# State-space work of a hybrid decoder step: loads three slots behind their stores, and state, output and gated products in one slot

## The chip, the cores and the metric

The kernel runs on one core of a Trainium2 chip. The metric is device time in microseconds (us); 1889.3 us is the median of three runs before the change, 1888.42 to 1891.9.

## The reference

One step of a decoder layer on 256 prompt tokens and 8 x 4 sample tokens, 288 token columns in all: a gated feed-forward block, a mixer of two branches side by side, and a second feed-forward block. The change is in the first branch, the state-space model (SSM), with 64 groups of 16 channels and 64 complex states each.

```python
x = x + 0.5 * swiglu(rms_norm(x, ffn1_norm), ffn1_w_gate, ffn1_w_up, ffn1_w_down)
u, q, k, v = split(rms_norm(x, mix_norm) @ w_in)
# SSM branch, s5_mixer:
bu = einsum('blgc,gpc->blgp', u, B_bar);  bu[:, 0] += lam_bar * h0
_, h = associative_scan(h_t = lam_bar * h_{t-1} + bu_t)
y = gelu(einsum('blgp,gcp->blgc', h, C).real + D * u)
y_ssm = y * sigmoid(einsum('blgc,gcd->blgd', y, w_glu))
# attention branch: sliding window of 128, 16 query heads on 4 key heads
x = x + w_out @ concat(rms_norm(y_ssm), rms_norm(y_attn))
x = x + 0.5 * swiglu(rms_norm(x, ffn2_norm), ...)
```

The last states h and the new key and value rows are outputs too.

## The kernel before

**Pieces and slots.** All large products read their weights in pieces of up to 512 KB. For each piece the weight is split into two parts (wh by ScalarE, line 104; wl by VectorE, line 105), and three products (lines 288 to 290) of 288 columns are made for each of 8 row blocks: 24 products a piece. Making one piece's products is a *slot*; the mixer's slots are counted here from its first piece (*base* = slot 0). Slots 0 to 39 are the input projection (two slots for each 128 columns: key, then eight pieces j = 0 to 7 of u, key, value twice, eight pieces of q), slots 40 to 71 the output projection.

**What sets the order.** Every engine runs its instructions in the order in which the program issues them. At the start of slot n, `W.next` issues the split of piece n+2 (wh and wl have three buffers each, so this split waits until the products of piece n-1 are through), the load of piece n+5 (raw, on the SP queue), and then the list of other work hung on slot n: `W.at(slot, f)` hangs one call on a slot, `W.spread(slot, gen)` runs one step of a generator in each slot from there on. Then come the slot's 24 products. So TensorE does the small products hung on slot n first and the 24 products after them, and VectorE does the wl of piece n+2 first and then the slot's other work. Calls hung before stand ahead of calls hung later; steps of a generator are hung when the step before has run.

**The SSM branch.** For each j, with s = base + 2j + 5: the projected u is scaled by VectorE (line 714) and stored to DRAM as ud (`ssm_u_store`, on ScalarE's queue), and loaded back in another layout as U (`ssm_u_load`, four DMAs on the SP queue). Tables are loaded from DRAM: ma (for the state), rot, mb (for the output), and the decay row D0 is built. `ssm_state` is a generator of four steps: (1) 8 products of U and ma (L748) and four VectorE products with rot (L754 to L757); (2) sums and the two scans (L760 to L766); (3) ScalarE and POOL prepare the rest, and VectorE rotates back into cs (L775, L776); (4) VectorE finishes cs (L778, L779). `ssm_out` makes 12 products from U, cs and mb (L788 to L790) and the gelu yg; `ssm_y_store` and `ssm_y_load` take it through DRAM (yd) into yn; `ssm_glu` makes the gated product (L809), a tanh, y2 (L814), and its split into hh and hl with the sum of squares acc (L699, L703). The norm of the branch (line 222 with ones and acc, then VectorE) gives R_ssm, which the output projection's results need from slot 40 on. `state_done` and `ssm_done` close pools whose memory the attention then uses; `cache_k_load` and `cache_v_load` load into it.

Each fp32 product of small tiles appears in the profile as two instructions (the 8 of L748 as 16). All PSUM tiles come from eight buffers named main.

Of the kernel before, what the change touches and what calls it, by code (L numbers as in the profile page):

```python
# [10 lines left out]
F32 = mybir.dt.float32  # L11
# [6 lines left out]
P = 128  # L18
# [6 lines left out]
W1 = NB + NCH  # L25
# [7 lines left out]
EPS = 1e-6  # L33
# [99 lines left out]
def tile_hymba_step(ctx, tc, io):  # L133
# [499 lines left out]
    with ExitStack() as es:  # L633
        mix(tc, nc, io, es, W, MIX0, dict(
            x=x, xh=xh, xl=xl, gains=gains, ident=ident, ones=ones, acc=acc, R=R, tp=tp,
            dr=dr, pm=pm, pa=pa, proj=proj, mm3=mm3, norm=norm, rsqrt=rsqrt, now=now, Hold=Hold,
            mats=mats, e4=e4, h4=h4, h0=h0, post=post_norm(32)))
# [9 lines left out]
def mix(tc, nc, io, es, W, base, e):  # L647
    act, dve, pool_e, pe = nc.scalar, nc.vector, nc.gpsimd, nc.tensor
    tt, ts, stt = dve.tensor_tensor, dve.tensor_scalar, dve.scalar_tensor_tensor
    x, R, gains, ident, acc = e["x"], e["R"], e["gains"], e["ident"], e["acc"]  # L650
# [6 lines left out]
    sa = sa_es.enter_context(tc.tile_pool(name="ssm_in", bufs=1, side="right", reuse_waits="tile"))  # L657
    sm = sb_es.enter_context(tc.tile_pool(name="ssm_out", bufs=1, reuse_waits="tile"))
    late = {}

    def aux():
        return pa.tile([P, 512], F32, name="main")
# [7 lines left out]
    R_ssm = mp.tile([P, N], F32, name="R_ssm")  # L670
# [16 lines left out]
    def y_split(pool, src, g, first, eng=pool_e):  # L687
        hh = pool.tile([P, N], F32R, name="hh", bufs=8)
        if first:
            pool.tile([P, 32], F32, name="gap_y", bufs=1)  # L690
        hl = pool.tile([P, N], F32R, name="hl", bufs=8)
        gc = gains[:, g:g + 1]
        act.activation(halved(hh), evens(src), AF.Copy, scale=gc)
        YH.append(hh)
        YL.append(hl)
        sq = tp.tile([P, N], F32, name="sq", bufs=3)
        act.activation(sq, src, AF.Square)
        yield
        stt(halved(hl), evens(src), gc, halved(hh.bitcast(F32)), op0=ALU.mult, op1=ALU.subtract)  # L699
        if first:  # L700
            eng.tensor_copy(acc, sq)
        else:
            eng.tensor_tensor(acc, acc, sq, op=ALU.add)  # L703


    MA, MB, ROT, D0, U, CS, UE, YG, YN, GL = ({} for _ in range(10))
    c4 = [P, 4, NCH]

    def flat(ap):
        return ap.rearrange("p q k -> p (q k)")  # L710
# [20 lines left out]
        get(ROT[j].rearrange("p q s k -> p (q s k)"), e["mats"][j][:, 2560:])  # L731

    def ssm_decay(j):
        D0[j] = sa.tile(c4, F32, name="d0", bufs=2)
        act.copy(D0[j], e["e4"][:, 4 * j:4 * j + 4, None].to_broadcast(c4))
        pool_e.memset(D0[j][:, :, 0:1], 0.0)

# [4 lines left out]
    def ssm_state(j):  # L742
        ma, u, rot = MA.pop(j), U[j], ROT.pop(j)
        b = []
        for i in range(2):
            ps = aux()
            for q in range(4):
                pe.matmul(ps[:, q * W1:(q + 1) * W1], ma[:, i, q], u[:, q], start=True, stop=True)  # L748
            b.append(ps[:, :N].rearrange("p (q t) -> p q t", q=4))
        br, bi = b[0][:, :, NB:], b[1][:, :, NB:]  # L750
        co, si = rot[:, :, 0, :], rot[:, :, 1, :]
        a1, a2, a3, a4 = (sa.tile(c4, F32, name="ra%d" % i, bufs=2) for i in range(4))
        q = slice(4 * j, 4 * j + 4)
        tt(a1, br, co, op=ALU.mult)  # L754
        tt(a2, bi, si, op=ALU.mult)
        tt(a3, bi, co, op=ALU.mult)
        tt(a4, br, si, op=ALU.mult)  # L757
        yield
        for i in range(2):
            tt(fin_s[:, i, q, :], b[i][:, :, :NB], fin_s[:, i, q, :], op=ALU.add)  # L760
        tt(a1, a1, a2, op=ALU.add)
        tt(a3, a3, a4, op=ALU.subtract)
        d0 = flat(D0.pop(j))
        zr, zi = a2, a4
        dve.tensor_tensor_scan(flat(zr), d0, flat(a1), 0.0, op0=ALU.mult, op1=ALU.add)
        dve.tensor_tensor_scan(flat(zi), d0, flat(a3), 0.0, op0=ALU.mult, op1=ALU.add)  # L766
        yield
        cs = CS[j] = sm.tile([P, 2, 4, W1 + 1], F32, name="cs", bufs=2)
        pool_e.memset(cs[:, :, :, NB:NB + 1], 0.0)
        act.copy(cs[:, 0, :, :NB], e["h0"][:, 0, q, :])  # L770
        act.copy(cs[:, 1, :, :NB], e["h0"][:, 1, q, :])
        sr, si_ = cs[:, 0, :, NB + 1:], cs[:, 1, :, NB + 1:]
        pool_e.tensor_tensor(a1, zi, si, op=ALU.mult)
        pool_e.tensor_tensor(a3, zr, si, op=ALU.mult)
        tt(sr, zr, co, op=ALU.mult)  # L775
        tt(si_, zi, co, op=ALU.mult)  # L776
        yield
        tt(sr, sr, a1, op=ALU.subtract)  # L778
        tt(si_, si_, a3, op=ALU.add)  # L779
        for i in range(2):  # L780
            pool_e.tensor_copy(fin[:, i, q], cs[:, i, :, W1])

    def ssm_out(j):
        mb, u, cs = MB.pop(j), U.pop(j), CS.pop(j)
        ps = aux()
        for q in range(4):
            o = ps[:, q * W1:(q + 1) * W1]
            pe.matmul(o, mb[:, 0, q], u[:, q], start=True, stop=False)  # L788
            pe.matmul(o, mb[:, 1, q], cs[:, 0, q, :W1], start=False, stop=False)  # L789
            pe.matmul(o, mb[:, 2, q], cs[:, 1, q, :W1], start=False, stop=True)  # L790
        YG[j] = sm.tile([P, 4, W1], F32, name="yg", bufs=1)
        act.activation(YG[j].rearrange("p q t -> p (q t)"), ps[:, :N], AF.Gelu_apprx_tanh)

    def ssm_y_store(j):
# [11 lines left out]
    def ssm_glu(j):  # L806
        yn = YN.pop(j)
        ps = aux()
        pe.matmul(ps[:, :N], GL.pop(j), yn, start=True, stop=True)  # L809
        t = tp.tile([P, N], F32, name="s1")  # L810
        act.activation(t, ps[:, :N], AF.Tanh, scale=0.5)
        yield
        y2 = tp.tile([P, N], F32, name="s2")
        stt(y2, t, 1.0, yn, op0=ALU.add, op1=ALU.mult)  # L814
        yield
        yield from y_split(ys, y2, 48 + j, j == 0, dve if j == 7 else pool_e)
# [14 lines left out]
    for j in range(8):  # L831
        s = base + 2 * j + 5
        W.at(s, ssm_u_store, j)
        W.at(s, ssm_load_a, j)
        W.at(s + 2, ssm_u_load, j)
        W.at(s + 2, ssm_decay, j)
        W.at(s + 2, ssm_load_r, j)
        W.spread(s + 4, ssm_state(j), True)
        W.at(s + 6, ssm_load_b, j)
        W.at(s + 9, ssm_out, j)  # L840
        W.at(s + 10, ssm_y_store, j)
        W.at(s + 11, ssm_y_load, j)
        W.spread(s + 13, ssm_glu(j))
    W.at(s + 8, state_done)
    W.at(s + 17, ssm_done)
    W.spread(s + 18, e["norm"](e["ones"], acc, R_ssm, 1.0 / 1024, 4 * EPS))

    def tok(ap, blk):

# [236 lines left out]
    for i in range(8):  # L1086
        s = base + 2 * (12 + i) + 2
# [3 lines left out]
        W.at(s + 11, pv, i)  # L1091
    for p in range(2):
        s = base + 2 * (12 + 4 * p + 3) + 2
        W.at(s - 4, cache_k_load, p)
        W.at(s + 4, cache_v_load, p)
        W.at(s, cache_gain, p)
        W.spread(s + 2, sample(p))
    for i in range(8):
        p, g = divmod(i, 4)
# [186 lines left out]
```

## Time and profile before

| | us |
|---|---|
| median of three runs | 1889.3 (1888.42 to 1891.9) |
| the profiled execution | 1890.48 |
| its span, first to last instruction | 1888.7 |
| TensorE (PE) busy in the span | 1864.6 |
| VectorE (DVE) busy | 1208.9 |
| ScalarE (ACT) busy | 850.2 |
| GpSimd (POOL) busy | 301.1 |
| mixer: start of slot 0, of slot 40 | 805.31, 991.98 |

Times in the profile count from the first instruction. A timeline row gives start, duration, engine, line, operation, result<-operands, shapes and count, and in brackets the engine's idle time before it with what ended it. A row of the waits gives engine and line, what was waited for, the total in us, how often, and the longest. A SPq or ACTq row is the issue of DMAs by that queue, and its duration includes what the queue waited for. Starts of two rows of one engine, subtracted, give the pace; a product's own duration overlaps with the next. Lines from 738 on carry the same numbers in both kernels up to L822; behind it the changed kernel's are 6 higher.

### The profile page before, as it was taken

To read this page: it belongs to the slowest core of one execution; us is meant where nothing else is said; L and a number is where in the kernel's file an instruction comes from. 1 tells how busy PE (TensorE), PEld (TensorE's weight loads), DVE (VectorE), ACT (ScalarE), POOL (GpSimd) and SP (SyncE) were. 2 spreads that over 40 slices of the span, in tenths; PEclk is the share of its full clock that TensorE was granted. 3 is DMA by queue.
4 is the path that set the end of the run, shared out by engine and by line. 5 is a ranking of instruction groups with operands and counts; after the bars stand their busy time and mean duration, and the time that the engine had idled before them with its cause. 6 is when DMAs were issued, how large, how long until landed. Compare 5 with 4: busy or idle time off the path is not lost.

```text
span 1888.7 us, 37634 instructions
## 1 busy us (share of the span) xinstructions
PE 1864.6 (99%) x15256; PEld 1850.5 (98%) x15256; DVE 1208.9 (64%) x1874; ACT 850.2 (45%) x1334; POOL 301.1 (16%) x450
## 2 busy tenths in 40 slices
PE   7999999999999999999999999999999999999999
PEld 7999999999999999999988999999999999999999
DVE  5677767666667755687788885555555555555555
ACT  6444444544444444643477554443444334434443
POOL 3111011000200100211378650000000000000000
PEclk9999999999999999999999999999999999999999
DMA  7565656557665765778743456555655565556555
GB/s 244 185 195 166 215 182 213 194 167 232 202 202 162 226 212 151 237 248 276 248 140 122 158 172 187 180 163 182 195 174 180 168 195 182 168 163 207 179 162 168
DMA packets 122623, 359.04 MB, mean 190 GB/s; under 512 B 22449, under 2 KB 30257, under 8 KB 121265
## 3 DMA queue, kind: packets, MB, share of 16 engines
q1 hardware_dynamic: 114672, 340.81, 57.6%
q10 hardware_dynamic: 7776, 15.83, 2.5%
q8 instruction: 119, 1.95, 0.4%
q14 instruction: 56, 0.45, 0.1%
HBM read 338.40 MB, written 20.22 MB: 190 GB/s over the span
## 4 chain that ended last, share of the span: by engine, by line
PE 92%; DVE 2%; POOL 2%; DMA 1%; ACT 1%; issue 1%; SPq 0%; POOLq 0%; ACTq 0%; DVEq 0%
PE main L288 30%; PE main L290 30%; PE main L289 29%; DVE wl L105 1%; ACT wh L104 1%; PE main L748 1%; DMA U<-ud 0%; DMA ud<-t 0%; POOL acc L206 0%; PE main L581 0%; PE main L587 0%; POOL x L1111 0%; DMA raw<-in_w_gu 0%; PE main L789 0%; PE main L790 0%
## 5 line engine op out<-in xcount | busy, mean ns | idle before, releaser
L105 DVE TENSOR_TENSOR wl<-raw,wh 128x1024 fp32r<-128x1024 f32 (+2 forms) x680 | 756.1, 1112 | 466.4 <-ACT wh L104 461.5
L288 PE MATMUL main<-xh,wh 128*128 128x288 f32 x3136 | 904.4, 288 | 7.0 <-ACT xh L196 6.4
L290 PE MATMUL main<-xh,wl 128*128 128x288 f32 x3136 | 898.6, 287 | 3.0 <-DVE wl L105 3.0
L289 PE MATMUL main<-xl,wh 128*128 128x288 f32 x3136 | 898.4, 286 | 0.6 <-DVE xl L197 0.6
L104 ACT CAST wh<-raw 128x1024 fp32r<-128x1024 f32 (+2 forms) x680 | 639.6, 942 | 510.4 <-PE main L289 349.7
L288 PEld LDWEIGHTS main<-xh,wh 128*128 128x128 f32 x3136 | 594.2, 189 | 8.6 <-ACT xh L196 6.4
L290 PEld LDWEIGHTS main<-xh,wl 128*128 128x128 f32 x3136 | 593.9, 189 | 3.9 <-DVE wl L105 3.9
L289 PEld LDWEIGHTS main<-xl,wh 128*128 128x128 f32 x3136 | 594.1, 189 | 1.4 <-DVE xl L197 0.9
L288 PE MATMUL main<-hh,wh 128*128 128x288 f32 x1664 | 478.0, 287 | 1.3 <-DVE t L1110 0.7
L289 PE MATMUL main<-hl,wh 128*128 128x288 f32 x1664 | 476.0, 286 | 0.6 <-DVE hl L699 0.6
L290 PE MATMUL main<-hh,wl 128*128 128x288 f32 x1664 | 476.0, 286 | 0.0
L288 PEld LDWEIGHTS main<-hh,wh 128*128 128x128 f32 x1664 | 314.5, 189 | 1.9 <-DVE t L1110 0.9
L289 PEld LDWEIGHTS main<-hl,wh 128*128 128x128 f32 x1664 | 314.5, 189 | 1.0 <-DVE hl L699 0.8
L290 PEld LDWEIGHTS main<-hh,wl 128*128 128x128 f32 x1664 | 314.5, 189 | 0.2 <-DVE wl L105 0.2
L315 POOL TENSOR_TENSOR s<-s,R 128x288 f32<-128x288 f32 x88 | 70.5, 801 | 1144.6 <-ACT s L314 1144.6
L314 ACT ACTIVATE s<-t 128x288 f32<-128x288 f32 x88 | 39.0, 443 | 220.8 <-DVE t L313 220.8
L324 ACT CAST hh<-h 128x288 fp32r<-128x288 f32 x88 | 38.0, 432 | 221.9 <-DVE h L323 221.9
L345 DVE SCALAR_TENSOR_TENSOR x<-main,x 128x288 f32<-128x288 f32 x128 | 58.4, 456 | 39.9 <-PE main L290 39.6
L323 DVE TENSOR_TENSOR h<-main,s 128x288 f32<-128x288 f32 x88 | 40.1, 455 | 55.5 <-PE main L290 55.1
L313 DVE TENSOR_TENSOR t<-main,R 128x288 f32<-128x288 f32 x88 | 40.1, 456 | 45.7 <-PE main L290 45.4
L325 DVE TENSOR_TENSOR hl<-h,hh 128x288 fp32r<-128x288 f32 x88 | 40.3, 458 | 43.8 <-ACT hh L324 43.8
L206 POOL TENSOR_TENSOR acc<-acc,sq 128x288 f32<-128x288 f32 x45 | 44.9, 999 | 41.5 <-ACT sq L202 40.1
(266 smaller groups left out, 901.3 us busy)
## 6 DMA issues: line engine op xcount, KB each, us to landing
raw<-in_w_gu SPq DMA_DIRECT2D x352, 512.0 KB, 3.8
raw<-in_w_dn SPq DMA_DIRECT2D x128, 384.0 KB, 3.1
raw<-in_w_dn SPq DMA_DIRECT2D x128, 320.0 KB, 3.1
raw<-in_w_in SPq DMA_DIRECT2D x40, 512.0 KB, 4.5
raw<-in_w_out SPq DMA_DIRECT2D x32, 512.0 KB, 3.4
mats<-stage ACTq DMA_DIRECT2D x8, 1536.0 KB, 7.2
mb<-mats SPq DMA_DIRECT2D x8, 768.0 KB, 7.0
ma<-mats SPq DMA_DIRECT2D x8, 512.0 KB, 4.1
```

What stands on the lines that cost most here:

```text
L104: self.nc.scalar.copy(wh[:, :n], t[:, :n])
L105: self.nc.vector.tensor_tensor(wl[:, :n], t[:, :n], wh[:, :n].bitcast(F32), op=ALU.subtract)
L206: eng.tensor_tensor(acc, acc, sq, op=ALU.add)
L288: pe.matmul(ps, wh[:, s], woven(rh[k]), start=first and a == 0, stop=False)
L289: pe.matmul(ps, wh[:, s], woven(rl[k]), start=False, stop=False)
L290: pe.matmul(ps, wl[:, s], woven(rh[k]), start=False, stop=last and a == n - 1)
L313: dve.tensor_tensor(t1, pg[:, :N], R, op=ALU.mult)
L314: act.activation(s1, t1, AF.Silu)
L315: pool_e.tensor_tensor(s2, s1, R, op=ALU.mult)
L323: dve.tensor_tensor(halved(h), evens(pu[:, :N]), evens(s2), op=ALU.mult)
L325: dve.tensor_tensor(hl, h, hh.bitcast(F32), op=ALU.subtract)
L345: dve.scalar_tensor_tensor(x[d], ps[:, :N], 0.5, x[d], op0=ALU.mult, op1=ALU.add)
```

## The change

The SSM's steps are hung on later slots. Relative to s: U's load moves from 2 to 3, ma from 0 to 4, rot from 2 to 5, the decay row from 2 to 6, the state's four steps from 4..7 to 6..9, mb from 6 to 8, the output from 9 to 10, yd's store from 10 to 11, yn's load from 11 to 14, the gated product's four steps from 13..16 to 16..19. The norm takes two slots (39 and 40) instead of four (37 to 40). D0 has one buffer instead of two, yg two instead of one; the attention's cache loads are one slot later.

```diff
-        D0[j] = sa.tile(c4, F32, name="d0", bufs=2)
+        D0[j] = sa.tile(c4, F32, name="d0", bufs=1)
...
-        YG[j] = sm.tile([P, 4, W1], F32, name="yg", bufs=1)
+        YG[j] = sm.tile([P, 4, W1], F32, name="yg", bufs=2)
...
         W.at(s, ssm_u_store, j)
-        W.at(s, ssm_load_a, j)
-        W.at(s + 2, ssm_u_load, j)
-        W.at(s + 2, ssm_decay, j)
-        W.at(s + 2, ssm_load_r, j)
-        W.spread(s + 4, ssm_state(j), True)
-        W.at(s + 6, ssm_load_b, j)
-        W.at(s + 9, ssm_out, j)
-        W.at(s + 10, ssm_y_store, j)
-        W.at(s + 11, ssm_y_load, j)
-        W.spread(s + 13, ssm_glu(j))
-    W.at(s + 8, state_done)
-    W.at(s + 17, ssm_done)
-    W.spread(s + 18, e["norm"](e["ones"], acc, R_ssm, 1.0 / 1024, 4 * EPS))
+        W.at(s + 3, ssm_u_load, j)
+        W.at(s + 4, ssm_load_a, j)
+        W.at(s + 5, ssm_load_r, j)
+        W.at(s + 6, ssm_decay, j)
+        W.at(s + 8, ssm_load_b, j)
+        W.at(s + 10, ssm_out, j)
+        W.at(s + 11, ssm_y_store, j)
+        W.at(s + 14, ssm_y_load, j)
+        W.spread(s + 16, ssm_glu(j))
+        W.spread(s + 6, ssm_state(j))
+    W.at(s + 10, state_done)
+    W.at(s + 18, ssm_done)
+
+    def ssm_norm():
+        for n, _ in enumerate(e["norm"](e["ones"], acc, R_ssm, 1.0 / 1024, 4 * EPS)):
+            if n == 1:
+                yield
+
+    W.spread(s + 20, ssm_norm())
...
-        W.at(s - 4, cache_k_load, p)
-        W.at(s + 4, cache_v_load, p)
+        W.at(s - 3, cache_k_load, p)
+        W.at(s + 5, cache_v_load, p)
```

What that does to the order is seen at three places. On VectorE, before, from the split of slot 12 to that of slot 13 (j = 0 in its fourth step, j = 1 in its second; the number behind ra tells them apart):

```order
L105 TENSOR_TENSOR wl<-raw,wh 128x1024
L778 TENSOR_TENSOR cs<-cs,ra_10473 128x4x64
L779 TENSOR_TENSOR cs<-cs,ra_10475 128x4x64
L760 TENSOR_TENSOR h_210<-main,h_210 128x32 x2
L761 TENSOR_TENSOR ra_10584<-ra_10584,ra_10585 128x256
L762 TENSOR_TENSOR ra_10586<-ra_10586,ra_10587 128x256
L765 SCALAR_TENSOR_TENSOR ra_10585<-d_10452,ra_10584 128x256
L766 SCALAR_TENSOR_TENSOR ra_10587<-d_10452,ra_10586 128x256
L105 TENSOR_TENSOR wl<-raw,wh 128x1024
```

The same stretch in the changed kernel, slot 14:

```order
L105 TENSOR_TENSOR wl<-raw,wh 128x1024
L760 TENSOR_TENSOR h_210<-main,h_210 128x32 x2
L761 TENSOR_TENSOR ra_10630<-ra_10630,ra_10631 128x256
L762 TENSOR_TENSOR ra_10632<-ra_10632,ra_10633 128x256
L765 SCALAR_TENSOR_TENSOR ra_10631<-d_10617,ra_10630 128x256
L766 SCALAR_TENSOR_TENSOR ra_10633<-d_10617,ra_10632 128x256
L778 TENSOR_TENSOR cs<-cs,ra_10528 128x4x64
L779 TENSOR_TENSOR cs<-cs,ra_10530 128x4x64
L105 TENSOR_TENSOR wl<-raw,wh 128x1024
```

The fourth step of j now stands behind the second step of j + 1. On TensorE, before, the end of slot 13 and the first output (j = 0, slot 14), followed by slot 14's own products:

```order
L290 MATMUL main<-xh_102,wl 128x288
L788 MATMUL main<-U,mb 128x72
L789 MATMUL main<-cs,mb 128x72
L790 MATMUL main<-cs,mb 128x72
L788 MATMUL main<-U,mb 128x72
L789 MATMUL main<-cs,mb 128x72
L790 MATMUL main<-cs,mb 128x72
```

And in the changed kernel the end of that first output, now in slot 15, with what follows it:

```order
L788 MATMUL main<-U,mb 128x72
L789 MATMUL main<-cs,mb 128x72
L790 MATMUL main<-cs,mb 128x72
L748 MATMUL main<-U,ma 128x72 x8
L288 MATMUL main<-xh_95,wh 128x288
L289 MATMUL main<-xl_112,wh 128x288
```

Before, a state (of j + 3) came one slot behind the output; now the state of j + 2 (L748) stands right behind it in the same slot. From j = 3 the gated product L809 of j - 3 stands ahead of the output (before, from j = 2, that of j - 2). On the SP queue, before, at the first U loads:

```order
L96 DMA raw<-in_w_in 128x1024 x2
L723 DMA U<-ud_10084 32x4x72 x4
L731 DMA rot<-mats_198 128x512
L727 DMA ma<-mats_199 128x1024
L96 DMA raw<-in_w_in 128x1024 x2
L723 DMA U<-ud_10085 32x4x72 x4
```

And in the changed kernel:

```order
L723 DMA U<-ud_10084 32x4x72 x4
L96 DMA raw<-in_w_in 128x1024
L727 DMA ma<-mats_198 128x1024
L96 DMA raw<-in_w_in 128x1024
L731 DMA rot<-mats_198 128x512
L723 DMA U<-ud_10085 32x4x72 x4
L96 DMA raw<-in_w_in 128x1024
```

A weight load now stands between any two groups of SSM loads, where two stood behind a longer group.

## The prediction

> **What bounds the kernel now.** First the page's busy shares, then who TensorE waited for.
>
> ```profile
> span 1888.7 us, 37634 instructions
> PE 1864.6 (99%) x15256; PEld 1850.5 (98%) x15256; DVE 1208.9 (64%) x1874; ACT 850.2 (45%) x1334; POOL 301.1 (16%) x450
> ```
>
> TensorE is busy for all but 24.1 us of the span, so a change that leaves its work alone acts only through its pauses. The table of its waits lists them:
>
> ```profile
> PE main L288 <- ACT xh L196: 6.4, 1, 6.4
> PE main L748 <- DMA U<-ud: 2.6, 3, 1.3
> PE main L748 <- DVE wl L105: 2.3, 1, 2.3
> PE main L990 <- POOL lg L942: 1.5, 2, 1.0
> PE main L961 <- DVE rq_v L1026: 1.4, 1, 1.4
> ```
>
> The 6.4 us are the start. The SSM's own share is the two rows of L748, the state product, which waits for its reloaded input U: 4.9 us. The attention (L990, L961) has about 3 us more.
>
> The third look is at windows of one slot each (columns: stretch, its length, busy time of each engine, granted clock, DMA share, GB/s): one slot of 24 main products, the state products of one j with nothing else, the output products of one j.
>
> ```profile
> 830.26:833.20 2.94, 2.94 (x27) 2.94 (x25) 2.87 (x6) 1.05 (x1) 0.00 (x0) 1.00 0.81 278
> 833.20:834.90 1.70, 1.70 (x18) 1.70 (x17) 1.67 (x3) 1.35 (x2) 0.10 (x1) 1.00 1.04 328
> 854.38:857.06 2.68, 2.68 (x28) 2.68 (x26) 2.36 (x5) 2.33 (x2) 0.00 (x0) 1.00 1.01 384
> ```
>
> So a slot of main products is 2.94 us, the state adds 1.70, the output about 2.6. These are TensorE's own time and the change keeps all of it. DMA is full here (1.01 to 1.04 in two of the three). The timelines of the SP queue and of TensorE, and the SP queue's waits, show why U is late:
>
> ```profile
> 850.75 8.20 SPq L723 DMA_DIRECT2D U<-ud  x4
> 860.00 0.86 SPq L96 DMA_DIRECT2D raw<-in_w_in  x2
> SPq L802 <- DMA yd<-yg: 16.8, 4, 6.6
> SPq L723 <- DMA ud<-t: 8.7, 2, 6.4
> 870.94 0.29 PE L290 MATMUL main<-xh,wl 128*128 128x288 f32 x1
> 873.55 2.51 PE L748 MATMUL main<-U,ma 128*128 128x72 f32 x16 [2.33 <-DVE wl L105]
> 875.81 0.59 PE L288 MATMUL main<-xh,wh 128*128 128x288 f32 x1
> ```
>
> SP issues the U load right after the store and stands on its landing (8.20 us for four issues), with weight loads queued behind. The worst result is the 2.33 us pause before 873.55. Its row names wl, but the other states don't wait for wl, and U was being loaded; I read it as U.
>
> **What the change removes.** U is now loaded three slots behind its store and used three slots later; yn likewise. SP runs ahead of TensorE, but the rot load, which now waits for VectorE's work on j - 3 and stands ahead of U in SP's order, holds it back to about one slot ahead; two slots then remain between the store and the load, 5.9 us of main products plus one group of SSM products, and three slots between the load and its use. The longest stand was 8.20 us, so I take the 4.9 us as gone. Each pause also costs a restart: the state that waited 0.97 us (row below) lengthened its slot from 845.59 to 851.44, 5.85 us against 2.94 + 1.70 = 4.64, so 0.24 more than the wait; four of these are 1.0. And the big pause was followed by a slow stretch:
>
> ```profile
> 849.66 1.98 PE L748 MATMUL main<-U,ma 128*128 128x72 f32 x16 [0.97 <-DMA U<-ud]
> 851.44 0.37 PE L288 MATMUL main<-xh,wh 128*128 128x288 f32 x1
> 871.40:874.82 3.42, 1.27 (x12) 1.30 (x12) 2.04 (x4) 1.53 (x4) 0.62 (x3) 1.00 1.06 291
> 874.82:878.23 3.41, 3.41 (x17) 3.41 (x17) 1.36 (x4) 0.00 (x0) 0.92 (x2) 0.50 0.95 308
> 878.23:881.65 3.42, 3.42 (x28) 3.24 (x27) 0.94 (x2) 1.35 (x2) 0.00 (x0) 1.00 0.99 340
> ```
>
> After 3.42 us in which TensorE was busy for 1.27, the granted clock was 0.50 for 3.41 us: 1.7 us lost. Removed in all: 4.9 + 1.0 + 1.7 = 7.6 us. Ends: 3.6 (if the pause at 873.55 is a wait for wl that stays) and 7.6.
>
> **What it adds: the output now follows its state's last step by one slot.** Before, L778 and L779 (the last step, which finishes cs) ran in slot s+7 and the output in s+9; now s+9 and s+10. And on VectorE the last step of j now stands behind the scan step of j+1 (L760 to L766), which stood behind it before. VectorE, ScalarE and TensorE in slot 12 of before:
>
> ```profile
> 845.59 0.29 PE L288 MATMUL main<-xh,wh 128*128 128x288 f32 x1
> 845.73 1.05 ACT L104 CAST wh<-raw 128x1024 fp32r<-128x1024 f32 x1 [2.51 <-PE main L289]
> 846.88 1.21 DVE L105 TENSOR_TENSOR wl<-raw,wh 128x1024 fp32r<-128x1024 f32 x1
> 848.01 0.41 DVE L778 TENSOR_TENSOR cs<-cs,ra 128x256 f32<-128x256 f32 x1
> 848.35 0.41 DVE L779 TENSOR_TENSOR cs<-cs,ra 128x256 f32<-128x256 f32 x1
> 848.68 0.27 DVE L760 TENSOR_TENSOR h<-main,h 128x32 f32<-128x32 f32 x2
> 850.15 0.66 DVE L766 TENSOR_TENSOR_SCAN ra<-d,ra 128x256 f32<-128x256 f32 x1
> 850.73 1.19 DVE L105 TENSOR_TENSOR wl<-raw,wh 128x1024 fp32r<-128x1024 f32 x1
> ```
>
> The weight split sets the clock of this queue: wh of piece n+2 waits until TensorE is through with the piece before this slot (ACT's row names L289), and wl follows wh. From that end (845.59) to wl is 1.29 us, wl takes 1.13 to the next start, the scan step 848.68 to 850.73 = 2.05, the last step 0.67 and 0.08 of tail: 5.22 us. TensorE has one slot of 2.94 us meanwhile, plus 0.1 for the output's first product, which needs no cs. It then waits 2.2 us. Nothing covers this: the state that could run meanwhile stands behind the output in TensorE's order.
>
> That is the wait for j = 0, 1, 2, 6.6 us. From j = 3 a gated product stands ahead of the output, worth 903.50 to 904.06, say 0.5; from j = 4 other VectorE work of the same slots stands ahead too:
>
> ```profile
> 903.50 0.72 PE L809 MATMUL main<-yn,gl 128*128 128x288 f32 x2
> 904.06 0.34 PE L788 MATMUL main<-U,mb 128*128 128x72 f32 x2
> L814 DVE SCALAR_TENSOR_TENSOR s<-s,yn 128x288 f32<-128x288 f32 x2 | 0.9, 451 | 0.0
> 919.36 0.45 DVE L214 SCALAR_TENSOR_TENSOR rt<-R_ssm 128x288 f32<-128x288 f32 x1
> 920.71 0.42 DVE L778 TENSOR_TENSOR cs<-cs,ra 128x256 f32<-128x256 f32 x1
> 981.01 0.45 DVE L226 TENSOR_SCALAR rv<-main 128x288 f32<-128x288 f32 x1
> 982.08 0.34 DVE L1050 SCALAR_TENSOR_TENSOR ls<-main,rq_b,ls 128x128 f32<-128x128 f32 x1
> ```
>
> j = 3: 2.2 - 0.5 = 1.7. j = 4: plus the start of a norm (981.01 to 982.08 = 1.07) and L814 (0.45), less 0.4 for the norm's product on TensorE: 2.8. j = 5: plus L814, one norm step (919.36 to 920.71 = 1.35), L699 (0.46, taken like L814) and about 0.4 by which VectorE comes late to wl, since the slot before holds a norm step also: 4.4. j = 6: plus L814 and L699: 2.6. j = 7 has no scan step ahead of it and a score product on TensorE: 0. Sum 6.6 + 1.7 + 2.8 + 4.4 + 2.6 = 18.1 us. Low end: with nothing but L778 and L779 behind wl the chain is 3.17 us and the wait 0.1 each, about 1 in all; the order excludes that, and 14 is as low as I go. High end 26, if POOL's work at the same time slows two VectorE operations in each chain to 1.0 us as in this row (0.41 elsewhere):
>
> ```profile
> 909.35 1.01 DVE L762 TENSOR_TENSOR ra<-ra,ra 128x256 f32<-128x256 f32 x1
> 986.77 0.45 DVE L214 SCALAR_TENSOR_TENSOR rt<-ri 128x288 f32<-128x288 f32 x1
> 986.11 0.33 PE L1003 MATMUL main<-pt,V 128*64 128x128 f32 x2
> ```
>
> **Slow clock.** The new pauses of 2.0 to 4.4 us are like the one that cost 1.7 us. Which of them fill enough of a 3.41 us stretch depends on where they fall; the pauses of 1.4 us and less in the table left it alone (this is the only slow stretch between the start and the end), 2.33 did not. I take two of seven: 3.4 us; ends 0 and 8.5. The Trainium skill ("TensorE: Matmul & The Clock Gate", Part 1 and the closing table) asks for an idle window of about 3.4 us before the clock is halved and says to avoid gaps over about 3 us; by it only j = 5 would pay, 1.7 us instead of 3.4, and the sum below would be 1903.0 instead of 1904.7. The trace disagrees: 2.33 us sufficed, so I don't go by it.
>
> **The moved norm.** The SSM norm's product (L222) moves from slot 37 to slot 39, where it is TensorE's first work and needs the last acc of slot 38. VectorE was late there: slot 38's first work started at 986.77, TensorE came to slot 39 at 986.11. L699 and acc take 0.9, so TensorE waits to 987.7: 1.5 us; ends 0 and 3. The norm's work in two bursts instead of four is the same work and ends in slot 40 as before.
>
> At nothing: D0 with one buffer (its copy waits for a scan one slot earlier, and ScalarE stands by for the output anyway), YG with two (ScalarE is 45% busy), the cache loads one slot later (their readers come two or more slots on), the SP queue's waits for ma and rot (weights are loaded five slots ahead of use, and SP is held to about one). The gated products' 0.9 us each on VectorE for j = 5 to 7 fall into the attention: ±2 us on its waits.
>
> **Sum** against the profiled execution, 1890.5 us (span 1888.7; 1.2 us above the median 1889.3): -7.6 + 18.1 + 3.4 + 1.5 = +15.4, so 1905.9; against the median 1904.7, say 1905.
>
> **Rivals.** (a) The loads win: if the state's last step came ahead of the output in time, only -7.6 remains: 1881.7. For it: U's rows. Against it: the order and the 5.22 us chain. It decides the sign if the eight output waits total under 7.6 us, 0.95 each. Chance 0.09. (b) A draw: the waits come to half (9 us), no slow clock: 1889.3 - 7.6 + 9 = 1891, chance 0.09 with its neighbours within 0.2% (3.8 us, about what a measurement here can tell from no change). (c) The loads don't help: DMA stays full, U or raw stays late, and the added waits come on top with four slow stretches: 1889.3 + 18.1 + 6.8 + 1.5 = 1915.7, chance 0.1. My forecast, slower by 4 to 25 us, has 0.72.
>
> Range: low 1889.3 - 7.6 + 14 - 4 = 1891.7; high from (c) 1916. Faster 0.09, same 0.09, slower 0.82.
>
> **What would show it.** In the profile after: waits of L789 for DVE cs L779, seven of 1.5 to 4.5 us, near 18 us in total; the two L748 rows gone; one to five stretches at clock 0.50 between 845 and 930 us; SP no longer standing on ud<-t and yd<-yg; a wait of L222 for DVE acc. I am wrong if L789 waits under 8 us, which would mean that VectorE reaches L779 before TensorE ends its slot, or if L748 still waits for U.

## The result, and the profile after

The changed kernel takes 1924.45 us (median of four runs, 1919.98 to 1924.94) against 1889.04 us beside it: a ratio of 1.0177, 95% interval 1.0165 to 1.0189. It is slower, as forecast, but by 35 us and not by 16, and the time lies above the range. The profiled execution is the shortest of the four, 1919.98 us; the other three show a mean clock of 0.986 to 0.987 against its 0.988.

The page of the changed kernel, the same rows as before and the row of the granted clock:

```profile
span 1918.2 us, 37617 instructions
PE 1884.9 (98%) x15256; PEld 1871.2 (98%) x15256; DVE 1201.7 (63%) x1874; ACT 850.3 (44%) x1334; POOL 303.3 (16%) x450
PEclk9999999999999999997799999999999999999999
```

The span grew by 29.5 us, but TensorE's *busy* time grew by 20.3 us with the same 15256 instructions: most of the loss is not waiting but products that ran slower. The clock row says where, in two of the 40 slices. The waits of TensorE hold the rest:

```profile
PE main L789 <- DVE cs L778: 13.8, 7, 3.3
PE main L222 <- DVE acc L703: 2.0, 1, 2.0
PE main L1042 <- DVE rq_v L1032: 1.9, 1, 1.9
```

Both L748 rows are gone, and seven waits of the output product L789 for VectorE's last state step have come. One of them, slot 16 on VectorE and the output of j = 1 behind it on TensorE:

```profile
864.95 1.23 DVE L105 TENSOR_TENSOR wl<-raw,wh 128x1024 fp32r<-128x1024 f32 x1 [0.50 <-ACT wh L104]
866.09 0.28 DVE L760 TENSOR_TENSOR h<-main,h 128x32 f32<-128x32 f32 x2
868.14 0.40 DVE L778 TENSOR_TENSOR cs<-cs,ra 128x256 f32<-128x256 f32 x1
868.46 0.41 DVE L779 TENSOR_TENSOR cs<-cs,ra 128x256 f32<-128x256 f32 x1
```
```profile
866.61 0.29 PE L290 MATMUL main<-xh,wl 128*128 128x288 f32 x1
866.73 0.34 PE L788 MATMUL main<-U,mb 128*128 128x72 f32 x2
868.68 0.41 PE L789 MATMUL main<-cs,mb 128*128 128x72 f32 x2 [1.61 <-DVE cs L778]
872.74 3.62 PE L748 MATMUL main<-U,ma 128*128 128x72 f32 x16
876.10 0.59 PE L288 MATMUL main<-xh,wh 128*128 128x288 f32 x1
879.84 0.33 PE L288 MATMUL main<-xh,wh 128*128 128x288 f32 x1
```

The scan step stands ahead of L778 as the order said, and TensorE, through with its slot at 866.7, waits 1.61 us. What follows is the surprise: from the start of the state product L748 to the next product 3.36 us pass (872.74 to 876.10) where 1.70 passed before, and the 15 main products from 876.10 to 879.84 take 3.74 us, 0.25 each, where a slot of 24 takes 2.94, 0.12 each. The windows around it (columns as before; the third value from the end, ahead of the DMA share, is the clock):

```profile
866.26:869.67 3.41, 1.80 (x16) 1.64 (x15) 3.41 (x9) 1.04 (x1) 1.07 (x1) 1.00 0.23 45
869.67:873.08 3.41, 3.41 (x18) 3.41 (x18) 0.34 (x1) 0.10 (x1) 0.52 (x2) 0.50 0.86 283
873.08:876.50 3.42, 3.42 (x18) 3.42 (x18) 0.53 (x2) 0.84 (x4) 1.51 (x4) 0.50 1.02 396
876.50:879.91 3.41, 3.41 (x16) 3.41 (x16) 1.65 (x5) 0.00 (x0) 0.00 (x0) 0.50 0.34 107
879.91:883.30 3.39, 3.39 (x29) 3.39 (x29) 1.62 (x3) 1.05 (x1) 0.00 (x0) 1.00 0.23 68
```

One pause of 1.61 us is followed by three stretches at half clock. TensorE is busy through all of them, in the first two almost only with the small products of the output and the state (L788 to L790, L748), and full clock returns only behind a stretch of main products. There are four such places: behind the outputs of j = 1, 2, 5 and 6, for 10.24, 10.24, 13.65 and 10.24 us, 44.4 us in all, of which half, 22.2 us, is lost (0.3 less, since TensorE also stands for 0.65 us in the first stretch of the third). They start whole multiples of 3.41 us apart (869.67, 886.74, 931.11 and 951.59: 5, 18 and 24 of them behind the first), so the stretches lie on a fixed grid, and it matters where on it a pause falls.

The account of the mixer, by the starts of its slots: slots 5 to 40 took 170.75 us before and 202.01 after, 31.3 us more. Gone are the waits for U with their restarts and slow stretch, 7.6 us by the starts of those slots against like slots without a wait; added are about 15 us at the seven outputs (13.8 of waits, the rest restarts), 22.2 us of slow clock, and what is left, some 1.6 us, at the norm and in the attention. Behind slot 40 the attention gives 1.8 us back.

### The profile page after: what moved, and what is told of

Its sections match the earlier page's. It is cut to its first block, busy times and chain, and to the rows that moved or that the text cites. A ratio compares the mean times of both kernels' runs of the same rounds, so it can differ in the third digit from the quotient of the medians.

```text
span 1918.2 us, 37617 instructions
## 1 busy us (share of the span) xinstructions
PE 1884.9 (98%) x15256; PEld 1871.2 (98%) x15256; DVE 1201.7 (63%) x1874; ACT 850.3 (44%) x1334; POOL 303.3 (16%) x450
## 4 chain that ended last, share of the span: by engine, by line
PE 48%; POOL 2%; DVE 1%; issue 0%; ACT 0%; POOLq 0%; ACTq 0%
PE main L288 15%; PE main L289 15%; PE main L290 15%; DVE wl L105 0%; POOL x L1117 0%; PE main L789 0%; PE main L790 0%; POOL rq_t L922 0%; PE main L977 0%; ACT wh L104 0%; POOL acc L703 0%; PE main L748 0%; PE main L788 0%; POOL lg L948 0%; POOL rq_t L920 0%
```

## The experiments

Three theories of the slow clock were told apart first: the pauses alone lower it (T1), the 4.3 us of small products standing together alone do (T2), or a pause lowers it and the small products behind hold it down (T3).

**The order on VectorE alone.** The change had also dropped the word `True` from the state's line. With it the generator's first step is hung behind the calls already on that slot, so the older j's steps come first, and L778 and L779 stand ahead of the next scan step again; TensorE's order stays. (The expectation of a later experiment calls this "in front of the older work"; it is behind.)

```diff
-        W.spread(s + 6, ssm_state(j))
+        W.spread(s + 6, ssm_state(j), True)
```

> The changed kernel with one word more: the state generator's first step is hung behind the steps that are already running, so that on VectorE the last step of j (L778, L779) stands ahead of the scan step of j + 1, as it did before the change. TensorE's order stays that of the changed kernel: output and state in one slot. Theory 1 (the pauses of L789 halve the clock): with a chain of 1.29 + 1.13 + 0.75 = 3.17 us against a slot of 2.94 the pauses nearly vanish, no stretch at clock 0.50 is left between 845 and 970 us, and the time falls by the pauses (about 15) and the clock (22): near 1886 us. Theory 2 (the 4.3 us of small products in one slot halve the clock, pause or not): the pauses go, the slow stretches stay, and the time is 1905 to 1910 us.

Measured: 1893.29 us, ratio 1.0026 [1.0014, 1.0037]. One flag takes back 31 of the 35 us; it stays 7 us above the 1886 of theory 1.

```profile
PE main L788 <- DMA mb<-mats: 1.3, 1, 1.3
PE main L789 <- DVE cs L778: 1.2, 1, 1.2
PE main L809 <- DMA gl<-in_w_glu: 0.7, 1, 0.7
```

The output waits once, for 1.2 us. Output and state still share a slot, in slots 14 to 19 at full clock: 7.32 + 3.02 us for each pair, so the small products by themselves don't lower it (against T2). The one slow place, 888.91 to 899.15, 5.1 us lost, stands behind the two new waits for DMA, of gl and mb:

```profile
885.50:888.91 3.41, 2.11 (x15) 1.68 (x16) 3.41 (x9) 0.66 (x2) 0.42 (x2) 1.00 1.04 363
888.91:892.32 3.41, 3.41 (x18) 3.41 (x18) 0.61 (x2) 0.72 (x3) 0.00 (x0) 0.50 0.81 246
```

**The output one slot later.** The wait is avoided the other way, and output and state no longer share a slot.

```diff
-        W.at(s + 10, ssm_out, j)
-        W.at(s + 11, ssm_y_store, j)
+        W.at(s + 11, ssm_out, j)
+        W.at(s + 12, ssm_y_store, j)
```

> The changed kernel with the output one slot later (s + 11) and its store at s + 12: the output is two slots behind the state's last step, and in the other slot than the state. Both theories: no wait of L789, no slow stretch. The loads' gain of 7.6 us remains, less the 2.0 us that the moved norm's product waits: 1889 - 7.6 + 2.0 = 1883.4 us. If the loads gained nothing, 1891 us.

Measured: 1891.35 us, ratio 1.0012 [1.0002, 1.0023]. L789 doesn't wait at all, so the mechanism of the added waits is shown from both sides. But the 7.6 us of the loads don't appear. TensorE now waits in their place:

```profile
PE main L748 <- ACT d L735: 2.4, 1, 2.4
PE main L748 <- issue: 1.7, 1, 1.7
PE main L748 <- DMA rot<-mats: 1.3, 1, 1.3
```

The row that names d, which L748 doesn't read, was probably a wait for the table ma: that was issued at 895.20, tables of this kind took 5.7 to 7.6 us to land here, and the product started at 902.60. Loading ma earlier (below) took the wait away.

**The same with the norm's steps behind the slot's other work** (`W.spread(s + 20, ssm_norm(), True)` on top).

> As the kernel with the output at s + 11, and the norm's first step is hung behind the slot's other work, so that TensorE has the probabilities' and queries' products of slot 39 (about 2 us) to do while VectorE finishes acc. Expected: L222 no longer waits, 2 us under the kernel with the output at s + 11: 1881.4 us. Rival: VectorE's late norm delays the first results of the output projection instead, and the time is the same as without it.

Measured: 1892.74 us, ratio 1.0017 [1.0006, 1.0027]. L222 no longer waits for acc, but a main product does, for line 1116, which scales the first result of the output projection with the late R_ssm:

```profile
PE main L288 <- DVE t L1116: 1.9, 1, 1.9
```

So the 2 us stay, as the rival said: this order only chooses where they are paid.

**Pauses and small products apart.** Four kernels are the kernel *before* with probes in the second feed-forward block, away from the SSM: at eight places ScalarE copies a tile and TensorE makes some fp32 products of 72 columns from it. If the copy is hung on the same slot, TensorE pauses for it by about 1.9 us; two slots earlier, it doesn't. Their outputs go nowhere.

```diff
+        held[i] = tp.tile([P, N], F32, name="sq", bufs=3)
+        act.copy(held[i], R)
...
+        for m in range(20):
+            o = 72 * (m % 4)
+            pe.matmul(ps[:, o:o + 72], s[:, 0:P], s[:, o:o + 72], start=True, stop=True)
...
+        W.at(n - 0, probe_fill, i)
+        W.at(n, probe, i)
```

A pause and one product (T1 expects slow stretches at most places):

> The kernel before, with a pause put at eight places of the second feed-forward block, five slots apart, among main products alone: at a slot's start one small product reads a copy that ScalarE makes in the same slot, behind the weight's cast, so TensorE stands for about 1.7 us. What is added is read by nothing. Theory 1 (a pause of this size halves the clock by itself, as my prediction assumed for some): two to six stretches at clock 0.50, and the time grows by 8 x 1.9 = 15 us and 1.7 us for each stretch. Theory 3 (a pause needs small products beside it): no slow stretch, 1889 + 15 = 1904 us.

No pause and 20 products:

> The same eight places of the kernel before, no pause, but 20 small products of 72 columns in one slot, as many as an output and a state together (4.3 us); their operand is ready two slots ahead. Theory 2 (the small products alone halve the clock): slow stretches at most of the eight places, each 3.4 us or more, and the time is over 1889 + 8 x 4.3 + 8 x 1.7 = 1937 us. Theories 1 and 3: clock 1.00 throughout, 1889 + 34 = 1923 us.

A pause and 20 products:

> The same eight places, pause and 20 small products together, as in the changed kernel. Theory 3 (the pause lowers the clock, the small products behind it hold it down): stretches of 10 us at 0.50 at several places, as in the changed kernel, five us lost at each: 1889 + 34 + 15 + 4 to 8 x 5 = 1958 to 1978 us. Theory 1: stretches as often as with the pause alone and as short, 3.4 us: near 1945 us.

A pause and 12 products:

> The kernel before with the eight pauses in the second feed-forward block and 12 small products behind each (2.6 us, an output alone) instead of 20. Theory 3 (the small products hold the clock down for as long as they last at half speed, 5.2 us here against 8.6): slow stretches of 3.4 to 6.8 us at some of the places, about 1.3 us less at each than with 20 products; 1891 + 21 + 16.6 + 4 to 8 x 2.5 = 1939 to 1949 us. If the number of small products doesn't matter: stretches as with 20, at seven places, 58 us in all: 1958 us.

Measured, single times against 1891.4 (the last: 1889.85): pauses alone 1908.57, small products alone 1923.39, both 1969.27, pause with 12 products 1944.95.

Pauses alone cost 17 us for eight, and one of eight places slowed, for one stretch:

```profile
PE main L653 <- ACT sq L646: 15.0, 8, 2.4
1140.83:1144.24 3.41, 1.27 (x11) 1.05 (x9) 1.64 (x4) 1.54 (x3) 0.00 (x0) 1.00 0.56 191
1144.24:1147.66 3.42, 3.21 (x13) 3.21 (x14) 1.09 (x1) 0.16 (x1) 0.00 (x0) 0.50 0.37 122
```

Small products alone cost 32 us, 160 of them at the 0.21 us that L748's take, and the clock stays full at the same place (the small products from 1141.48 to 1145.79):

```profile
1140.00:1147.00 7.00, 7.00 (x63) 7.00 (x62) 3.12 (x4) 1.38 (x2) 0.00 (x0) 1.00 0.47 166
```

Both together cost 78 us, where 17 + 32 make 49. The same pauses (15.0 us, eight) now slowed seven of eight places, for 6.83 or 10.24 us each, 58.0 us in all and 29 lost, which is the difference:

```profile
1143.10:1146.50 3.40, 1.68 (x15) 1.68 (x16) 1.69 (x2) 1.67 (x3) 0.00 (x0) 1.00 0.34 137
1146.50:1149.91 3.41, 3.41 (x18) 3.41 (x18) 0.00 (x0) 0.00 (x0) 0.00 (x0) 0.50 0.39 154
1149.91:1153.33 3.42, 3.42 (x17) 3.42 (x17) 0.00 (x0) 0.00 (x0) 0.00 (x0) 0.50 0.00 0
1153.33:1156.74 3.41, 3.41 (x16) 3.41 (x15) 0.00 (x0) 0.00 (x0) 0.00 (x0) 0.50 0.02 5
1156.74:1160.15 3.41, 3.41 (x30) 3.41 (x29) 1.23 (x1) 1.04 (x1) 0.00 (x0) 1.00 0.00 0
```
```profile
1144.82 7.31 PE L653 MATMUL main<-sq 128*128 128x72 f32 x40 [2.36 <-ACT sq L646]
1151.88 0.59 PE L288 MATMUL main<-xh,wh 128*128 128x288 f32 x1
```

The small products end at 1151.88, and the clock comes back only behind the window of main products that starts at 1153.33. With 12 products the slow places last 3.41 or 6.83 us (six of eight, 34.1 us): fewer small products, a shorter hold. So it takes the pause and the small products together to slow most places, and the small products hold the clock down, away from the SSM and its DMAs.

But they do more than T3 says: they also bear on whether a pause lowers the clock at all. A hold alone would make the slow places longer, not more (one of eight, then seven). Three of the lone pauses left a stretch with 1.66 to 1.68 us of work, most of it main products, and the clock stayed full; the first row below is one. With 20 small products, stretches with 1.06 to 2.45 us of work, nearly all small products, were followed by 0.50 at all seven places. The changed kernel shows the same. The pauses of j = 1 and 2 left stretches of 1.80 us of work, two thirds or more of it small products, and lowered the clock; those of j = 3 and 4 (the other two rows) left 1.54 and 1.70, about three quarters of it products of 288 columns, and did not; that of j = 0 fell across two stretches (2.21 and 3.01 us of work).

```profile
1178.38:1181.79 3.41, 1.67 (x13) 1.67 (x14) 1.23 (x1) 1.69 (x3) 0.79 (x1) 1.00 0.38 137
900.39:903.80 3.41, 1.54 (x12) 1.29 (x10) 3.41 (x9) 1.36 (x2) 0.00 (x0) 1.00 0.45 99
914.04:917.46 3.42, 1.70 (x13) 1.48 (x12) 3.39 (x12) 1.35 (x2) 0.19 (x1) 1.00 0.99 286
```

The probes are one execution each, and the SSM's own slow stretch came and went in them (none with small products alone); the counts are of the eight places only.

**Loading later.** Where did the loads' 7.6 us go? One idea was that SP still stands on buffers freed late, so that loading everything later would let it run. U, rot and yn go one slot later on the first experiment's kernel (e4_last_loads, here), and rot, mb and yn one slot, U two slots later on the second's (e5_out11_loads); both have the norm's steps behind slot 39's other work, so neither changes the loads alone.

```diff
-        W.at(s + 3, ssm_u_load, j)
-        W.at(s + 5, ssm_load_r, j)
-        W.at(s + 14, ssm_y_load, j)
+        W.at(s + 4, ssm_u_load, j)
+        W.at(s + 6, ssm_load_r, j)
+        W.at(s + 15, ssm_y_load, j)
...
-    W.spread(s + 20, ssm_norm())
+    W.spread(s + 20, ssm_norm(), True)
```

> The kernel with the state's step last (output and state in one slot, no pauses), its norm hung behind slot 39's other work, and three loads one slot later: U at s + 4, rot at s + 6, yn at s + 15. Their buffers are then free two slots before SP issues them instead of one. In the kernel with the state's step last, the waits for gl and mb (0.7 and 1.3 us, with one slow stretch of 10.24 us behind them) are the loads' new waits. Theory L (SP is held by buffers that VectorE and TensorE free late, so the tables come late): these waits and the slow stretch go, and the time is 1893.3 - 2.0 - 5.1 - 2.0 = 1884 us. Rival (the DMA engines themselves are full there): the tables stay late and the time is 1889 to 1892 us.

> The kernel with the output at s + 11, norm hung behind slot 39's other work, U at s + 5, rot at s + 6, mb at s + 9, yn at s + 15: buffers again free two slots before the load. Theory L: its 5.4 us of L748 waits go, 1892.7 - 6 = 1887 us or less. Rival: DMA full, waits stay, 1892 us.

Measured: 1900.18 us (1.0062 [1.0049, 1.0074]) and 1895.27 us (1.0029 [1.0018, 1.0039]), the one clearly worse than the kernel that it is built on, the other no better. The idea falls in that form: what is loaded later comes late. In the first it is rot, for which VectorE waits (first row), and the output waits for VectorE again, 5.9 us at four outputs, with a slow place of 10.24 us there. In the second the state again waits for what is loaded (the other rows; this profile is of its longest execution, 1900.42 us):

```profile
DVE ra L754 <- DMA rot<-mats: 14.7, 5, 6.1
PE main L748 <- DMA U<-ud: 3.3, 2, 1.9
PE main L748 <- DMA rot<-mats: 2.1, 1, 2.1
```

**Loading the tables earlier.** The change shortens the tables' lead: ma is loaded two slots ahead of its use where it was four, rot one where it was two, mb two where it was three. With ma at s + 2 and rot at s + 4, on the first experiment's kernel (e6_last_early, there also mb at s + 7) and on the second's (e7_out11_early):

```diff
-        W.at(s + 4, ssm_load_a, j)
-        W.at(s + 5, ssm_load_r, j)
+        W.at(s + 2, ssm_load_a, j)
+        W.at(s + 4, ssm_load_r, j)
```

> The changed kernel with the state's steps hung in front of the older work again (VectorE's last step ahead of the next scans) and with the tables loaded earlier: ma at s + 2, rot at s + 4, mb at s + 7 in place of s + 4, s + 5, s + 8. Theory (tables loaded too few slots ahead of their use are what takes the place of the removed waits for U): the waits of L788 on mb and of L809 on gl and the 10.24 us slow stretch behind them go, so about 1893.3 - 2.0 - 5.1 = 1886 us, ratio 0.998. Rival (DMA is full in these slots, or SP is held by stores, so something comes late wherever the tables stand): the waits move to other loads and the time stays at 1890 to 1894 us.

> The changed kernel with the output one slot later (s + 11, yd's store s + 12) and with ma at s + 2 and rot at s + 4 in place of s + 4 and s + 5. Theory (tables loaded too late): the waits of L748 on d and rot and without a named cause (5.4 us together) go, so about 1891.4 - 5 = 1886 us, ratio 0.998. Rival (DMA full or SP held): the L748 waits stay or turn into waits for other loads, 1890 to 1893 us.

Measured: 1897.49 us (1.0042 [1.003, 1.0055]) and 1891.26 us (1.0002 [0.9993, 1.0011]). In both TensorE's waits for tables are gone, and another load is late instead, the gated product's gl, by 5.88 us in the one and by 0.93 and 2.20 in the other. In the first the SP queue shows why:

```profile
877.69 9.70 SPq L723 DMA_DIRECT2D U<-ud  x4
887.49 0.38 SPq L96 DMA_DIRECT2D raw<-in_w_in  x1
887.91 0.43 SPq L802 DMA_DIRECT2D yn<-yd  x1
888.38 0.43 SPq L804 DMA_DIRECT2D gl<-in_w_glu  x1
```
```profile
891.69 1.33 PE L809 MATMUL main<-yn,gl 128*128 128x288 f32 x2 [5.88 <-DMA gl<-in_w_glu]
```

SP comes to a U load at 877.69 whose store is issued only at 878.22, and there it stands for 9.70 us (8.0 of them for ud<-t) with gl behind it. That the tables, loaded late, had held SP back from running so far ahead is inferred from this. That is the stand of the kernel before (8.20 us) in another place. The time of the first is 11 us above its forecast; against it stand this wait, 5.9 us, and the slow clock behind it, some 7 (17.07 us at 0.50, in 2.9 of which TensorE stood).

**gl ahead of the U load**, on the second kernel:

```diff
+        W.at(s + 13, ssm_gl_load, j)
         W.at(s + 14, ssm_y_load, j)
```

> e7_out11_early with gl, the gated product's weight, loaded at s + 13, in front of the next U load in SP's order, in place of s + 14 behind it. Theory (what is left of the removed waits stands in front of loads that come late): the two waits of L809 on gl (0.93 and 2.20 us in slots 20 and 22) and the one slow stretch behind the second go, 3.1 + 0.5 + 1.7 = 5 us, so about 1891.3 - 5 = 1886 us, ratio 0.998 and the first version below the kernel before. Rival (DMA is full there, so something else comes late in its place): waits of L748 or L788 on a table appear and the time stays at 1889 to 1892 us.

Measured: 1889.6 us, ratio 0.9999 [0.999, 1.0008], level with the kernel before and not the 1886 of the theory. The waits for gl are gone, but something else is late in part, as the rival said, the gated product's other operand:

```profile
PE main L811 <- DMA yn<-yd: 2.0, 2, 1.2
```

Most of the loads' gain is now seen: slots 5 to 32 take 126.38 us where the kernel before takes 132.69, 6.3 us less, or 5.2 like with like, since two gated products (1.1 us) have moved behind slot 32. Between slots 32 and 40 it is given back, 44.06 against 38.06: a pause in the attention, as long as in the changed kernel (1.9 us), where it left the clock alone (2.06 us of work in its stretch), slows it here (1.48):

```profile
961.00:964.41 3.41, 1.48 (x14) 0.97 (x12) 1.60 (x4) 3.41 (x8) 2.65 (x10) 1.00 0.31 119
964.41:967.82 3.41, 3.41 (x27) 2.60 (x27) 3.24 (x11) 1.36 (x4) 2.59 (x11) 0.50 0.54 156
967.82:971.24 3.42, 3.42 (x17) 3.42 (x16) 1.51 (x4) 3.19 (x13) 3.23 (x7) 0.50 0.34 98
```
```profile
964.05 0.41 PE L1045 MATMUL main<-kG,qs 64*128 64x32 f32 x2 [1.85 <-DVE rq_v L1035]
964.38 1.10 PE L1049 MATMUL main<-ck,qs 64*32 64x256 f32 x16
965.42 1.02 PE L970 MATMUL main<-mcst,qsq 128*128 128x2 f32 x4
```

That is 3.4 us lost; waits of 0.8 us at the norm and of 1.9 in the attention, and the moved gated products, stand against most of the rest. It was not tried to take that pause away too. No version here beats the kernel before.

## Why the prediction was right and wrong

**The waits of the output: right in cause, somewhat too long.** Seven waits of L789 for VectorE's last step, none for j = 7. Predicted 18.1 us, measured 13.8 (1.61, 1.61, 1.61, 2.08, 1.73, 3.28, 1.93 for j = 0 to 6; predicted 2.2 three times, then 1.7, 2.8, 4.4, 2.6). For j = 1 the chain is 1.16 + 1.14 + 2.05 + 0.54 = 4.89 us against the 5.22 of the working: the scan step fits, the ends were shorter. And the output's first product covers 0.34 us, not 0.1. The flag that restores the order takes away all but 1.2 us of the waits, the output one slot later takes all.

**Slow clock: the step that failed.** The working took two of seven pauses at one stretch of 3.41 us each, 3.4 us, and 8.5 as the high end. Four of seven slowed it, and for three or four stretches each: 22.2 us, 18.8 too few in the sum. The step took every pause for the same kind of event as the one row that it went by, a pause of 2.33 us and one slow stretch. That stretch held about 1 us of the state's small products (874.82 to 875.81) and then main products, so it was short for a reason that I didn't ask for. In the changed kernel 4.3 us of small products stand behind the pause, 8.6 us at half clock (for j = 6, which has no state behind it, the output's 2.6 and some of the attention's). The probes show that these hold the clock down, and that a pause lowers it more readily with such products in its stretch: so both the length of a slow place and the number of them were too low. With 22.2 in place of 3.4 and 13.8 in place of 18.1, the working's own sum would have been 1889.3 - 7.6 + 13.8 + 22.2 + 1.5 = 1919.2, near the profiled 1919.98. The median is 5 us more; the other three executions left no trace, but their mean clock, 0.001 to 0.002 lower, makes 2 to 4 us over 1920 (an estimate). The rival (c), nearest in time with 1915.7, was not right in its cause, since the loads did help.

**A short pause and the clock.** The rule of the Trainium skill ("TensorE: Matmul & The Clock Gate", Part 1 and the closing table) asks for an idle window of about 3.4 us. It was set aside for the right reason, a short pause that slowed the clock, and the result speaks against it more strongly: here 1.61 us within a stretch of 3.41 us sufficed.

**What the change removes: right here.** Both L748 rows are gone, and U is never late: 7.6 us by the starts of the slots, as predicted. What I had not seen is that, once the pauses and slow stretches were taken away, tables and gl came late; that the slow TensorE had given them the time is the likely reading, not shown by a run of its own. "At nothing" for the SP queue's waits was right of this kernel, wrong of its faster neighbours. The sign that SP would no longer stand on stores failed: at the U loads it stood on ud<-t for 5.1 us (8.7 before) and, by its rows, on yd<-yg for 14.0, though TensorE waited for none of these.

**The moved norm:** 2.0 us against 1.5. **The attention:** 1.9 us at L1042 against 1.4 at L961 before, within the ±2.

**The sign and the cases.** Slower had the most weight, for the reason that proved right. The high end failed since (c) priced four slow stretches at 1.7 us each, as if a pause could buy only one; there were thirteen.

## What to carry to other kernels

Look at what stands behind a pause on TensorE, not only at its length: the same 1.9 us cost about 2 us ahead of main products and about 5.7 ahead of 20 small fp32 products. (That is 78 less 32 us over eight places.) A step that a product needs must stand ahead of the neighbours' later steps on its engine; here that order hung on one word in the list of calls, and leaving it out, with the output moved to one slot behind that step, cost 31 us. Loads that leave early aren't safe on an in-order queue: each must also stand ahead of the loads that will stop it.

## What was not expected of the hardware

After a stretch of 3.41 us in which TensorE idled for 1.0 to 3.0 us, the granted clock was often 0.50 for the next one. With main products in the busy part 1.27 us of work was followed by it and 1.66 to 1.68 was not; with 20 small products behind the pause 1.68 to 2.45 us of them were followed by it, and with 12 in one case 2.68 us was not. A pause of 1.9 us mostly passed when main products stood on both sides (seven of eight), and mostly did not with 20 small products behind it (one of eight passed). Once lowered, the clock stayed at 0.50 through stretches that were busy from end to end with fp32 products of 72 columns, and was full again behind a stretch of main products, in the probes also behind some that held about 1.9 us of them, beside small ones. The same small products never lowered it by themselves (eight times 20, clock 1.000 over the whole run). Small products seem to count for less per us than main ones; where the threshold lies, and whether it goes by columns, by products or by something else, stays open.
